# A transformer layer on one core: output inputs turned by DMA transposes instead of TensorE, output scales and last tile's products on other steps

## The chip, the cores and the metric

The kernel runs on one core of one Trainium2 chip. Its time is the device time of one execution in microseconds; before the change the median of three runs is 2656.93 us (2654.02 to 2658.84). The core has TensorE (PE in the profile; its weight loads are PEld), VectorE (DVE), ScalarE (ACT), GpSimd (POOL) and SyncE (SP), which issues nearly all DMAs of this kernel on one queue.

## What is computed

The reference is one layer of a hybrid transformer, batch 1, sequence 2048, model width 1024, and a final norm:

```python
h = _modulate(_rmsnorm(x, norm1_g), sh1, sc1)
rq, rk, rv, rg, aq, ak, av = jnp.split(h @ w_in, SPLIT_IDX, axis=-1)
...
ret, _, _ = _bidir_retention(rq_h, rk_h, _heads(rv, RET_HEADS), log_gamma, s_f, s_b)
ret = _ret_out(ret, rg, ret_gn_g)
...
att = _latent_attention(q.reshape(B, L, ATT_KV_HEADS, ATT_GROUP, ATT_HD), k, v, kc, vc)

x = x + g1 * (jnp.concatenate([ret, att], axis=-1) @ w_out)

h2 = _modulate(_rmsnorm(x, norm2_g), sh2, sc2)
x = x + g2 * _sqrelu_mlp(h2, w_ff1, w_ff2)
```

The change sits at the product with `w_out`. Its left factor is, for each row of 128 positions, 512 values of the retention (`ret`) and 512 of the attention (`att`).

## The kernel before, in words

Three stages follow each other. A projection stage (to about 606 us) makes queries, keys, values and gates, and prepares scales; the rows of the later modulation are summed there by `later_rows` at the steps of the list `at` (L1260). An attention stage (about 606 to 1470 us) computes attention, retention and the output product together. An MLP stage does the two feed-forward products to the end.

The attention stage is written out by hand: `on(k, phase, fn)` files a piece of work under step k and a phase, and the main loop runs the steps in order and in each step the phases in the order of `PHASES`: scores, piece, maximum, early, exp, cast, low, chain, pe, values, late, dma. Every engine's queue has its instructions in that order and executes them in order. A step handles one block of 128 keys of one attention group: TensorE makes the scores (`st`, L210 and L211) and a piece of the next group's row maxima (`mp`, L177 or L181); VectorE reduces that piece (`nm`, L190); ScalarE takes the exponential (L216) and in every second step casts two blocks to float16 (`phi`, L220); the float16 remainder (`plo`) is made by GpSimd (L227) or in two halves by VectorE (L229); three steps later TensorE does the product with the values (L243, L245). There are two banks for `st` and two for `mp`, so TensorE can be two blocks ahead of ScalarE and VectorE and no more.

A group takes 18 steps, a tile of 128 positions 36 steps (`RF`), and 16 tiles run from the last position to the first; tile 0 is done last (`last` in `output_tile`). Work that belongs to a tile is filed relative to its step k, and runs on into the next tile's steps. `retention` makes the retention of a tile in steps k+2 to k+20 (`mask`, L1659, in step k+4 on VectorE, from bank 0) and ends in `rets`; `combine` puts the attention of the tile into `ats` in step k+25 (L262, L263, GpSimd).

`output_tile` then does, for all but the last tile:

- `transpose`: TensorE turns the four 128x128 blocks of `ret` in step k+24 and those of `att` in step k+28 (L1812, against `ident`, float32), into a PSUM bank;
- `part`: ScalarE writes the float16 high part from that bank (`rh` in step k+26, `ah` in k+30, phase cast, L1818), VectorE the low part (`rl` in k+27, L1822; `al` in k+31, L1820; phase early), reading the bank and the high part;
- `product`: 16 pieces of three 512-column products each (L1830, L1831, L1832) at the steps `PLACES`; the first eight, for the first 512 output columns, in k+28 to k+35, the first four of them on `r`, the next four on `a`; the other eight in k+46 to k+57;
- `add` (VectorE, L1837), `square` (ScalarE, L1844), `store_x`, `root`, `norm` (GpSimd, L1857), and in steps k+68 to k+77 the transposes `transpose_x` (L1862), `modulate` (L1867), `shift_` (L1872) and the stores of the MLP's input.

The last tile uses the steps `LAST`; what its next stage needs is moved out of the events into `rest`, which the main loop of the MLP stage takes two at a time. `output_scales` (L1759) takes the largest values over all partitions and derives the scales `gns`, `sco` and `inv`, in steps 22 to 26, before the first tile (`R0` is 40). SyncE's DMAs of a step are filed in its phase dma and are issued in order; a DMA that waits for a tile holds those behind it.

Of the kernel before, what the change touches and what calls it, by code (L numbers as in the profile page):

```python
# [11 lines left out]
F32 = mybir.dt.float32  # L12
F32R = mybir.dt.float32r
F16 = mybir.dt.float16
# [42 lines left out]
def layer_kernel(ctx: ExitStack, tc: tile.TileContext, a: dict, out: bass.AP):  # L57
# [212 lines left out]
    with ExitStack() as st, tc.manual_schedule():  # L270
# [90 lines left out]
        def later_rows(j, use, at):  # L361


            x = {}

            def load(i, k):
                w = x[i, k] = raw("wmo")
                src = a["w_mod"][0, k * P : (k + 2) * P, (j + i) * 512 : (j + i + 1) * 512]
                nc.sync.dma_start(w, src.rearrange("(k p) n -> p k n", p=P))

            def add(i, k):
                w = x.pop((i, k))
                if k == 0:
                    x["acc", i] = mq.tile([P, 512], F32, name="macc", tag="mb", bufs=2)
                for r in range(2):
                    c, acc = cc[:, k + r, :1], x["acc", i]
                    if k + r == 0:
                        nc.vector.tensor_scalar_mul(acc, w[:, r], c)
                    else:
                        nc.vector.scalar_tensor_tensor(acc, w[:, r], c, acc, op0=ALU.mult, op1=ALU.add)  # L380

            def bias(i):
                if i == 0:
                    x["b"] = op.tile([P, 512], F32, name="mrow", tag="mrow", bufs=1)
                src = a["b_mod"][0, (j + i) * 512 : (j + i + 1) * 512]
                nc.sync.dma_start(x["b"][32 * i : 32 * i + 32], src.partition_broadcast(32))

            def sums(i):
                if i == 0:
                    x["ps"] = psM.tile([P, 512], F32, name="mps", tag="mps")  # L390
                mm(x["ps"][32 * i : 32 * i + 32], ones, x["acc", i], start=True, stop=True)

            def end():
                b = x["b"]
                nc.vector.tensor_tensor(b[:64], x["ps"][:64], b[:64], op=ALU.add)

            for i in range(2):
                for k in range(0, KT, 2):
                    s = at.pop(0)
                    do(s - 1, "load", load, i, k)  # L400
                    do(s, "aux", add, i, k)
                do(s + 2, "turn", sums, i)
# [854 lines left out]
        for s, (g, col, m) in enumerate(units):  # L1257
            post(s, g, col, *GROUPS[g][m], done[s])

        at = [16, 17, 18, 19, 20, 20, 21, 21, 22, 22, 39, 40, 41, 42, 44, 46, 48, 50, 52, 54, 56, 58, 60, 62]  # L1260
        at += [66, 67, 68, 69, 70, 72, 74, 76]
        for j, use in ((4, store_gate(0)), (6, turn_rows(shift2)), (8, turn_rows(scale2)), (10, store_gate(1))):
            later_rows(j, use, at)
        at = [39, 40, 41] + list(range(43, 64, 2)) + list(range(66, 84))
# [331 lines left out]

    room = ctx.enter_context(ExitStack())
    rp = pool(room, "rp", side="right")
    BUFS = {"orv": 3, "ork": 2, "okw": 2, "oo": 2, "sf": 2, "sb": 2, "ma": 2}
    wo = rp.tile([P, KT, 2, D], F16, name="wo")  # L1600

    def room_tile(tag, dtype=F32, shape=(P, 512)):
# [6 lines left out]
    def retention(k0):  # L1609
# [94 lines left out]
        for n, (d, c) in enumerate(todo):  # L1704
            k = k0 + SF * n
            on(k - 5, "dma", take, c, "rk", "rv")
            on(k - 2, "late", weigh, d, c)
            on(k, "pe", product, c, n % 2, (0, 1))
            on(k + 1, "pe", product, c, n % 2, (2, 3))
            if d == 0:  # L1710
                old, to, tag = ("f" if c == STATES else "s", c - 2), ("s", c - 1), "sf"
            else:
                old, to, tag = None if c == 1 else ("b", NT), ("b", NT - 1 + c), "sb"
            on(k + 1, "late", update, d, c, old, to, tag, (0, 1))
            on(k + 2, "late", update, d, c, old, to, tag, (2, 3))
            if d == 0:
                on(k + 3, "dma", keep_state, c - 1)
        assert k0 + SF * len(todo) <= R0
        for n in range(NT):
            c, k = NT - 1 - n, R0 + RF * n  # L1720
# [36 lines left out]
    def output_scales(k):  # L1757

        x = {}  # L1759

        def greatest():
            w = room_tile("oat")
            x["y"], x["t"], x["one"], x["m"] = w[:, :1], w[:, 1:2], w[:1, 4 : 4 + P], w[:1, 2:3]
            nc.vector.memset(x["one"], 1.0)
            nc.vector.tensor_reduce(x["y"], wmx[:, 72:], axis=AX.X, op=ALU.max, apply_absolute_value=True)

        def turn():
            x["ps"] = bank(1)
            nc.tensor.transpose(x["ps"][:1, 0], x["y"], ident)

        def whole():
            nc.vector.tensor_reduce(x["m"], x["ps"][:1, 0], axis=AX.X, op=ALU.max)

        def spread():
            x["ps"] = bank(1)
            mm(x["ps"][:, 0, :1], x["one"], x["m"], start=True, stop=True)

        def scales():
            y, t = x["y"], x["t"]
            nc.vector.tensor_copy(y, x["ps"][:, 0, :1])  # L1780
            binade(y)


            nc.vector.tensor_scalar_mul(y, y, 2.0**-10)
            nc.vector.tensor_tensor(y, y, inv, op=ALU.max)
            nc.vector.tensor_tensor(gns[:, 0:1], y, y, op=ALU.mult)
            nc.vector.tensor_scalar_mul(gns[:, 1:2], gns[:, 0:1], EPS)
            nc.vector.tensor_tensor(sco, sci[:, 7:8], y, op=ALU.mult)
            nc.vector.reciprocal(t, y)
            nc.vector.tensor_tensor(inv, inv, t, op=ALU.mult)  # L1790

        on(k, "late", greatest)
        on(k + 1, "pe", turn)
        on(k + 2, "early", whole)
        on(k + 3, "pe", spread)
        on(k + 4, "early", scales)

    PLACES = (28, 29, 30, 31, 32, 33, 34, 35, 46, 48, 49, 50, 52, 54, 55, 57)
    LAST = (23, 24, 25, 26, 30, 31, 32, 33, 31, 31, 32, 32, 34, 34, 35, 35)

    def output_tile(t, k, last):
        y = {}

        def fetch_x():
            y["x"] = xp.tile([P, D], F32, name="xr", tag="xr", bufs=XR)
            nc.sync.dma_start(y["x"], a["x"][0, t * P : (t + 1) * P, :])

        def transpose(w):
            src = (rets if w == "r" else ats).pop(t)
            y["ps"] = bank(1)  # L1810
            for q in range(4):
                nc.tensor.transpose(y["ps"][:, q], src[:, q * P : (q + 1) * P], ident)  # L1812

# [9 lines left out]

        def product(n, k):
            if k == 0:
                y["acc", n] = bank(n if last else 0, (P, 512))
            w = "ra"[k // 4]
            hi, lo = y[w, 0][:, k % 4], y[w, 1][:, k % 4]
            wh, wl = (wo[:, k, i, n * 512 : (n + 1) * 512] for i in range(2))
            mm(y["acc", n], hi, wh, start=k == 0, stop=False)  # L1830
            mm(y["acc", n], hi, wl, start=False, stop=False)  # L1831
            mm(y["acc", n], lo, wh, start=False, stop=k == KT - 1)  # L1832
# [6 lines left out]
        def square(n):  # L1839
            if n == 0:  # L1840
                y["ss"] = sm.tile([P, 2], F32, name="ss", tag="ss")
            c = slice(n * 512, (n + 1) * 512)
            junk = room_tile("oat")
            nc.scalar.activation(junk, y["x"][:, c], AF.Square, accum_out=y["ss"][:, n : n + 1])  # L1844

        def store_x():
# [10 lines left out]
            nc.gpsimd.tensor_scalar(y["x"], y["x"], y["r"], 1.0, op0=ALU.mult, op1=ALU.mult)  # L1857

        def transpose_x(q):
            y["ps", q] = bank(q if t < 2 else 1)  # L1860
            for i in range(4):
                nc.tensor.transpose(y["ps", q][:, i], y["x"][:, (4 * q + i) * P : (4 * q + i + 1) * P], ident)  # L1862

# [10 lines left out]
        def store_h(q):  # L1874
            nc.sync.dma_start(h2_d[t][:, 4 * q : 4 * q + 4], y["u", q])

        steps = (20, 21, 22, 27, 28, 30) if last else (24, 26, 27, 28, 30, 31)
        for w, at in zip("ra", (steps[:3], steps[3:])):
            on(k + at[0], "pe", transpose, w)
            on(k + at[1], "cast", part, w, 0)  # L1880
            on(k + at[2], "early", part, w, 1)
        on(k + 26, "dma", fetch_x)
        places = LAST if last else PLACES
        for j, at in enumerate(places):
# [59 lines left out]
    done = attention()  # L1944
    retention(26)
    output_weights(30)
    output_scales(22)
    for n, t in enumerate(range(NT - 1, -1, -1)):
        made_at = output_tile(t, R0 + RF * n, n == NT - 1)
    for j in range(4):  # L1950
# [447 lines left out]
    with tc.manual_schedule():  # L2398
        for k in range(min(events)[0], max(events)[0] + 1):
            for phase in PHASES:  # L2400
                run(k, phase)
                if phase in ("maximum", "low", "late"):
                    link()
        assert not events and not chain
        up_jobs()
        down_jobs()
        k = min(events)[0]
        while events:
            for phase in FPHASES:
# [67 lines left out]
```

## Time and profile before

| what | before |
|---|---|
| median of 3 runs | 2656.93 us |
| profiled execution, its own time | 2656.33 us |
| its span | 2654.5 us |
| TensorE busy in the span | 98% |
| VectorE / GpSimd / ScalarE busy | 77% / 66% / 57% |
| share of the 16 DMA engines that SyncE's queue takes | 54.8% |
| period of a tile (from one `store_x` to the next, 780 to 993 us) | 53.2 us |

The span is the time from the first to the last instruction; the execution's own time has 1.8 us beside it. A row of a timeline reads: start in us from the span's start, duration in us, engine, line of the kernel, operation, out<-in, shape, count, and in brackets the idle time of the engine before it with what ended it. Matmul rows show a modelled end; the time a matmul really costs is the distance to the next start (0.22 us for 512 columns of float16). In the list of DMAs the last number is the median time from issue to landing.

### The profile page before, as it was taken

Reading aid. Unit: us, or ns where it says so; the run is one execution under the profiler, and the core shown is the slowest. Engines: PE = TensorE matmul, PEld = TensorE weight load, DVE = VectorE, ACT = ScalarE, POOL = GpSimd, SP = SyncE. Lnnn points to the kernel's source line nnn. Section 1 sums busy time; section 2 is a strip of 40 time slices with the busy share of each in tenths; the row PEclk is TensorE's granted clock in tenths of the full one; section 3 lists DMA queues with packets and bytes.
Section 4 is the critical chain, followed back from the end, with each engine's and each line's share of the span. In section 5 each row is a group of like instructions: output and inputs, shape, how many; then the busy total and the mean of one; then the engine's idle time right before and its main releaser. Section 6 shows DMA issues by size and latency. Waiting matters only on the chain.

```text
span 2654.5 us, 45435 instructions
## 1 busy us (share of the span) xinstructions
PE 2601.0 (98%) x16617; PEld 1450.9 (55%) x16617; DVE 2049.4 (77%) x3099; ACT 1504.7 (57%) x2544; POOL 1761.7 (66%) x1451
## 2 busy tenths in 40 slices
PE   8999999998999999999999999999999999999998
PEld 5875555545666666666666444444444444444443
DVE  5778798677888888988987597889876656655686
ACT  3856343425877778788878575666665322222243
POOL 3644566545676668888887696677662666666686
PEclk9999999999999999999999999999999999999999
DMA  7876899746022123333422754776685757475453
GB/s 231 272 252 207 303 330 323 257 119 218 25 84 72 57 65 116 96 84 92 128 77 80 259 170 150 230 241 231 208 297 144 278 180 287 165 293 174 160 187 114
DMA packets 332903, 481.84 MB, mean 182 GB/s; under 512 B 90228, under 2 KB 200068, under 8 KB 328200
## 3 DMA queue, kind: packets, MB, share of 16 engines
q1 hardware_dynamic: 332664, 478.94, 54.8%
q8 instruction: 130, 2.13, 0.3%
q14 instruction: 93, 0.76, 0.1%
q10 hardware_dynamic: 16, 0.01, 0.0%
HBM read 321.89 MB, written 156.38 MB: 180 GB/s over the span
## 4 chain that ended last, share of the span: by engine, by line
PE 69%; ACT 3%; POOL 2%; DVE 1%; DMA 1%; issue 0%; SPq 0%; POOLq 0%; DVEq 0%; ACTq 0%
PE pd L2290 7%; PE pd L2289 7%; PE pd L2288 7%; PE pu L2063 7%; PE pu L2061 7%; PE pu L2062 7%; PE st L210 4%; PE o L245 4%; PE st L211 4%; PE mp L177 3%; PE o L243 2%; PE bank L1832 2%; PE bank L1830 2%; PE bank L1831 2%; ACT p L216 1%; ACT phi L220 1%
## 5 line engine op out<-in xcount | busy, mean ns | idle before, releaser
L190 DVE TENSOR_REDUCE nm<-mp 128x1 f32<-128x512 f32 x558 | 377.6, 685 | 90.7 <-PE mp L177 85.4
L216 ACT ACTIVATE p<-st 128x512 f32<-128x512 f32 x576 | 341.4, 600 | 162.7 <-PE st L211 156.3
L227 POOL TENSOR_TENSOR plo<-p,phi 128x1024 f16<-128x1024 f32 x160 | 348.2, 2181 | 87.1 <-ACT phi L220 87.0
L2063 PE MATMUL pu<-hf,w1f 128*128 128x512 f16 x896 | 339.6, 379 | 0.0
L2290 PE MATMUL pd<-w,uf 128*128 128x512 f16 x896 | 339.6, 379 | 0.0
L2061 PE MATMUL pu<-hf,w1f 128*128 128x512 f16 x896 | 339.6, 379 | 0.0
L2289 PE MATMUL pd<-w,uf 128*128 128x512 f16 x896 | 339.6, 379 | 0.0
L2062 PE MATMUL pu<-hf,w1f 128*128 128x512 f16 x896 | 339.6, 379 | 0.0
L2288 PE MATMUL pd<-w,uf 128*128 128x512 f16 x896 | 339.6, 379 | 0.0
L2308 POOL TENSOR_TENSOR y<-y,d 128x512 f32<-128x512 f32 x128 | 210.4, 1646 | 146.6 <-ACT uf L2277 99.9
L220 ACT ACTIVATE phi<-p 128x1024 f16<-128x1024 f32 x288 | 305.2, 1060 | 0.0
L229 DVE TENSOR_TENSOR plo<-p,phi 128x512 f16<-128x512 f32 x256 | 240.1, 939 | 21.8 <-ACT phi L220 9.4
L243 PE MATMUL o<-wv,plo 128*128 128x65 f16 x2304 | 230.7, 193 | 0.3 <-POOL plo L227 0.2
L245 PE MATMUL o<-wv,phi 128*128 128x129 f16 x2176 | 229.0, 220 | 0.0
L210 PE MATMUL st<-qr,ks 128*128 128x512 f16 x576 | 218.3, 379 | 8.6 <-ACT p L216 6.3
L243 PEld LDWEIGHTS <-plo 128*128 128x128 f16 x2304 | 205.5, 98 | 30.4 <-POOL plo L227 2.4
L2300 DVE SCALAR_TENSOR_TENSOR y<-pd,scy,y 128x512 f32<-128x512 f32 x160 | 116.9, 747 | 132.3 <-PE pd L2290 132.1
L211 PE MATMUL st<-qr,ks 128*128 128x512 f16 x576 | 218.5, 379 | 0.0
L2073 DVE TENSOR_TENSOR r<-pu,r 128x512 f32<-128x512 f32 x224 | 150.0, 684 | 82.8 <-PE pu L2063 58.3
L1191 PE MATMUL pso<-wf,h_l 128*128 128x512 f16 (+1 forms) x576 | 208.2, 361 | 0.0
L1192 PE MATMUL pso<-wf,h_l 128*128 128x512 f16 (+1 forms) x576 | 208.1, 361 | 0.0
L1193 PE MATMUL pso<-wf,h_l 128*128 128x512 f16 (+1 forms) x576 | 208.1, 361 | 0.0
(389 smaller groups left out, 6116.2 us busy)
## 6 DMA issues: line engine op xcount, KB each, us to landing
wm<-in_w_ff SPq DMA_DIRECT2D x64, 512.0 KB, 7.1
u<-r SPq DMA_DIRECT2D x128, 256.0 KB, 4.4
ur<-u SPq DMA_DIRECT2D x128, 256.0 KB, 5.9
y<-x SPq DMA_DIRECT2D x64, 512.0 KB, 6.5
wf<-w2f SPq DMA_DIRECT2D x112, 256.0 KB, 2.9
w<-wf SPq DMA_DIRECT2D x28, 1024.0 KB, 10.0
w1r<-in_w_ff SPq DMA_DIRECT2D x48, 512.0 KB, 5.3
x<-y SPq DMA_DIRECT2D x48, 512.0 KB, 2.6
```

What stands on the lines that cost most here:

```text
L190: nc.vector.tensor_reduce(dst, src, axis=AX.X, op=ALU.max, negate=True)
L216: nc.scalar.activation(self.p[kt // 2][:, kt % 2], self.s.pop(kt), AF.Exp, scale=HD**-0.5)
L220: nc.scalar.activation(hi, self.p[j], AF.Copy)
L227: nc.gpsimd.tensor_tensor(lo, p, hi, op=ALU.subtract)
L243: mm(o[:, : HD + 1], lo[:, i, c], v[:, : HD + 1], start=False, stop=False)
L245: mm(o, hi[:, i, c], v[:, :VW], start=False, stop=last)
L2061: mm(pu[hf, i], whi, hi, start=k == 0, stop=False)
L2062: mm(pu[hf, i], whi, lo, start=False, stop=False)
L2063: mm(pu[hf, i], wlo, hi, start=False, stop=k == 3)
L2288: mm(ps, u[:, 0, b], w[:, b, 0], start=b == 0, stop=False)
L2289: mm(ps, u[:, 0, b], w[:, b, 1], start=False, stop=False)
L2290: mm(ps, u[:, 1, b], w[:, b, 0], start=False, stop=b == 3)
```

## The change

For all tiles but the last, the two TensorE transposes go. ScalarE and VectorE now write the float16 high and low parts of `ret` and `att` as rows, from SBUF to SBUF, in `rows`, and SyncE turns each of the four 128x512 float16 tiles by a DMA transpose, in `turn`. The casts keep their steps for `a` (k+30, k+31) and for `r` (k+26, k+27); the transposes are issued in the phase dma of the same steps, and `rh`, `rl`, `ah`, `al` are now written by DMA. The first eight products move three steps on, to k+31 to k+38, and with them their `add` (to k+39) and `square`. Banks 0 and 1 change roles in `product` and `transpose_x`. The tag `oo` has one buffer instead of two, a tag `rows` is new.

The last tile keeps its TensorE transposes. Four of its products for the second half move from steps 31 and 32 to 25 to 28, so that they lie around the transposes of `a`, whose low part is now made in phase low of step 28 instead of phase early of step 30; its bank comes from the MLP's pool.

`output_scales` starts at step 39 instead of 22, and its nine small VectorE operations are spread over steps 43 to 50, those with a second tensor replaced by a multiplication with a per-partition scalar. `keep_state` is issued one step earlier, `rest` is served after the phase pe instead of late, and in `later_rows` some of the additions move by one to three steps and the two sums are made together.

```diff
-            def sums(i):
-                if i == 0:
-                    x["ps"] = psM.tile([P, 512], F32, name="mps", tag="mps")
-                mm(x["ps"][32 * i : 32 * i + 32], ones, x["acc", i], start=True, stop=True)
+            def sums():
+                ps = psM.tile([P, 512], F32, name="mps", tag="mps")
+                for i in range(2):
+                    mm(ps[32 * i : 32 * i + 32], ones, x["acc", i], start=True, stop=True)
+                x["ps"] = ps
...
-        at = [16, 17, 18, 19, 20, 20, 21, 21, 22, 22, 39, 40, 41, 42, 44, 46, 48, 50, 52, 54, 56, 58, 60, 62]
-        at += [66, 67, 68, 69, 70, 72, 74, 76]
+        at = [16, 17, 18, 19, 20, 20, 21, 21, 24, 25, 39, 40, 41, 42, 44, 46, 49, 50, 52, 54, 56, 58, 60, 62]
+        at += [66, 67, 68, 69, 70, 71, 72, 73]
...
-    BUFS = {"orv": 3, "ork": 2, "okw": 2, "oo": 2, "sf": 2, "sb": 2, "ma": 2}
+    BUFS = {"orv": 3, "ork": 2, "okw": 2, "oo": 1, "sf": 2, "sb": 2, "ma": 2}
...
-                on(k + 3, "dma", keep_state, c - 1)
+                on(k + 2, "dma", keep_state, c - 1)
...
         def scales():
-            y, t = x["y"], x["t"]
-            nc.vector.tensor_copy(y, x["ps"][:, 0, :1])
-            binade(y)
-
-
-            nc.vector.tensor_scalar_mul(y, y, 2.0**-10)
-            nc.vector.tensor_tensor(y, y, inv, op=ALU.max)
-            nc.vector.tensor_tensor(gns[:, 0:1], y, y, op=ALU.mult)
-            nc.vector.tensor_scalar_mul(gns[:, 1:2], gns[:, 0:1], EPS)
-            nc.vector.tensor_tensor(sco, sci[:, 7:8], y, op=ALU.mult)
-            nc.vector.reciprocal(t, y)
-            nc.vector.tensor_tensor(inv, inv, t, op=ALU.mult)
-
-        on(k, "late", greatest)
+            y, t, mul = x["y"], x["t"], nc.vector.tensor_scalar_mul
+            later = [
+                lambda: nc.vector.tensor_copy(y, x["ps"][:, 0, :1]),
+                lambda: binade(y),
+                lambda: nc.vector.tensor_scalar(y, y, 2.0**-10, inv, op0=ALU.mult, op1=ALU.max),
+                lambda: mul(gns[:, 0:1], y, y),
+                lambda: mul(gns[:, 1:2], gns[:, 0:1], EPS),
+                lambda: mul(sco, sci[:, 7:8], y),
+                lambda: nc.vector.reciprocal(t, y),
+                lambda: mul(inv, inv, t),
+            ]
+            for i, fn in enumerate(later):
+                on(k + 4 + i, "late", fn)
+
+        on(k, "early", greatest)
...
-    PLACES = (28, 29, 30, 31, 32, 33, 34, 35, 46, 48, 49, 50, 52, 54, 55, 57)
-    LAST = (23, 24, 25, 26, 30, 31, 32, 33, 31, 31, 32, 32, 34, 34, 35, 35)
+    PLACES = (31, 32, 33, 34, 35, 36, 37, 38, 46, 48, 49, 50, 52, 54, 55, 57)
+    LAST = (23, 24, 25, 26, 30, 31, 32, 33, 25, 26, 27, 28, 34, 34, 35, 35)
...
+        def rows(w, i):
+            if i == 0:
+                y[w] = (rets if w == "r" else ats).pop(t)
+                y[w, "rows"] = room_tile("oat" if w == "r" else "rows", F16, (P, 2, 512))
+            row = y[w, "rows"]
+            scale = inv if w == "a" else 1.0
+            if i == 0:
+                nc.scalar.activation(row[:, 0], y[w], AF.Copy, scale=scale)
+            elif w == "a":
+                nc.vector.scalar_tensor_tensor(row[:, 1], y[w], scale, row[:, 0], op0=ALU.mult, op1=ALU.subtract)
+            else:
+                nc.vector.tensor_tensor(row[:, 1], y[w], row[:, 0], op=ALU.subtract)
+
+        def turn(w, i):
+            y[w, i] = room_tile(w + "hl"[i], F16, (P, 4, P))
+            nc.sync.dma_start(y[w, i], y[w, "rows"][:, i], transpose=True)
+
...
-                y["acc", n] = bank(n if last else 0, (P, 512))
+                y["acc", n] = bank(n if last else 1 - n, (P, 512))
...
-            y["ps", q] = bank(q if t < 2 else 1)
+            y["ps", q] = bank(q if t < 2 else 0)
...
-        steps = (20, 21, 22, 27, 28, 30) if last else (24, 26, 27, 28, 30, 31)
-        for w, at in zip("ra", (steps[:3], steps[3:])):
-            on(k + at[0], "pe", transpose, w)
-            on(k + at[1], "cast", part, w, 0)
-            on(k + at[2], "early", part, w, 1)
+        for w, at in (("r", 20), ("a", 27)) if last else (("r", 26), ("a", 30)):
+            if last:
+                on(k + at, "pe", transpose, w)
+                on(k + at + 1, "cast", part, w, 0)
+                on(k + at + (2 if w == "r" else 1), "early" if w == "r" else "low", part, w, 1)
+            else:
+                on(k + at, "cast", rows, w, 0)
+                on(k + at, "dma", turn, w, 0)
+                on(k + at + 1, "early", rows, w, 1)
+                on(k + at + 1, "dma", turn, w, 1)
...
-    output_scales(22)
+    output_scales(39)
...
-                if phase == "late" and rest:
+                if phase == "pe" and rest:
```

More of the change, by code (lines that the diff above doesn't have):

```diff
@@ L401, in later_rows @@
                     do(s, "aux", add, i, k)
-                do(s + 2, "turn", sums, i)
+            do(s + 2, "turn", sums)
             for i in range(2):
@@ L1761, in greatest @@
         def greatest():
-            w = room_tile("oat")
+            w = vp.tile([P, P + 4], F32, name="os")
             x["y"], x["t"], x["one"], x["m"] = w[:, :1], w[:, 1:2], w[:1, 4 : 4 + P], w[:1, 2:3]
@@ L1795, in output_scales @@
         on(k + 3, "pe", spread)
-        on(k + 4, "early", scales)
-    PLACES = (28, 29, 30, 31, 32, 33, 34, 35, 46, 48, 49, 50, 52, 54, 55, 57)
-    LAST = (23, 24, 25, 26, 30, 31, 32, 33, 31, 31, 32, 32, 34, 34, 35, 35)
+        on(k + 3, "late", scales)
+    PLACES = (31, 32, 33, 34, 35, 36, 37, 38, 46, 48, 49, 50, 52, 54, 55, 57)
+    LAST = (23, 24, 25, 26, 30, 31, 32, 33, 25, 26, 27, 28, 34, 34, 35, 35)
     def output_tile(t, k, last):
@@ L1806, in fetch_x @@
             nc.sync.dma_start(y["x"], a["x"][0, t * P : (t + 1) * P, :])
+        def rows(w, i):
[13 more added lines that the diff above has]
+            nc.sync.dma_start(y[w, i], y[w, "rows"][:, i], transpose=True)
         def transpose(w):
             src = (rets if w == "r" else ats).pop(t)
-            y["ps"] = bank(1)
+            y["ps"] = ff["ps"].tile([P, 4, P], F32, "aps") if last and w == "a" else bank(1)
             for q in range(4):
@@ L1842, in square @@
             c = slice(n * 512, (n + 1) * 512)
-            junk = room_tile("oat")
+            junk = room_tile("oat" if n or last else "rows")
             nc.scalar.activation(junk, y["x"][:, c], AF.Square, accum_out=y["ss"][:, n : n + 1])
```

## Prediction

> **What bounds the kernel now.** I began with the page, whose first lines give each engine's share.
>
> ```profile
> PE 2601.0 (98%) x16617; PEld 1450.9 (55%) x16617; DVE 2049.4 (77%) x3099; ACT 1504.7 (57%) x2544; POOL 1761.7 (66%) x1451
> ```
>
> TensorE is busy nearly always, so a reader would pay the change for the TensorE time that it removes. That must be read in the stage where the transposes lie; next, then, the busy time by stretches: TensorE, weight loads, VectorE, ScalarE, GpSimd, clock, DMA.
>
> ```profile
> 800.00:900.00 100.00, 99.09 (x962) 66.30 (x959) 85.19 (x159) 78.94 (x132) 67.28 (x60) 1.00 0.25 75
> 1470.00:1480.00 10.00, 7.26 (x27) 2.90 (x26) 4.36 (x4) 2.74 (x4) 8.12 (x7) 0.83 1.00 407
> ```
>
> The steady tiles (first row) look bound by TensorE, with DMA idle for three quarters. But 85 and 79% are means over a tile of 36 steps, so I took one tile's timelines, engine by engine. TensorE in steps k+24, k+28 and k+31:
>
> ```profile
> 835.02 0.60 PE L1812 MATMUL bank<-ident,oo 128*128 128x128 f32 x4
> ...
> 840.22 0.60 PE L1812 MATMUL bank<-ident,ma 128*128 128x128 f32 x4
> 840.66 0.38 PE L1830 MATMUL bank<-wo,rh 128*128 128x512 f16 x1
> ...
> 845.02 0.38 PE L181 MATMUL mp<-ks,qr 128*128 128x256 f16 x2
> 845.24 0.38 PE L1830 MATMUL bank<-wo,rh 128*128 128x512 f16 x1
> ```
>
> Four transposes cost 840.66 - 840.22 = 0.44 us of TensorE. ScalarE in the same stretch:
>
> ```profile
> 833.57 1.05 ACT L220 ACTIVATE phi<-p 128x1024 f16<-128x1024 f32 x1
> 834.51 0.62 ACT L1844 ACTIVATE oat<-xr 128x512 f32<-128x512 f32 x1
> ...
> 842.43 0.68 ACT L1818 ACTIVATE ah<-bank,inv 128x512 f16<-128x512 f32 x1
> 843.99 0.60 ACT L216 ACTIVATE p<-st 128x512 f32<-128x512 f32 x1 [0.88 <-PE st L211]
> ```
>
> No row between 833.57 and 843.11 carries an idle time: ScalarE runs through, and waits for TensorE again only after `ah`. So from step k+24 to k+30, just where both groups of transposes lie, ScalarE sets the pace and TensorE's transposes fill holes. VectorE, and GpSimd beside it:
>
> ```profile
> 838.70 0.69 DVE L1822 TENSOR_TENSOR rl<-bank,rh 128x512 f16<-128x512 f32 x1
> 839.31 0.68 DVE L190 TENSOR_REDUCE nm<-mp 128x1 f32<-128x512 f32 x1
> 840.13 1.47 DVE L229 TENSOR_TENSOR plo<-p,phi 128x512 f16<-128x512 f32 x1
> 841.52 0.68 DVE L190 TENSOR_REDUCE nm<-mp 128x1 f32<-128x512 f32 x1
> 842.12 0.92 DVE L229 TENSOR_TENSOR plo<-p,phi 128x512 f16<-128x512 f32 x1
> 842.97 0.68 DVE L190 TENSOR_REDUCE nm<-mp 128x1 f32<-128x512 f32 x1
> 844.14 0.69 DVE L190 TENSOR_REDUCE nm<-mp 128x1 f32<-128x512 f32 x1 [0.50 <-PE mp L177]
> ```
>
> ```profile
> 837.83 2.13 POOL L227 TENSOR_TENSOR plo<-p,phi 128x1024 f16<-128x1024 f32 x1
> 839.95 1.12 POOL L1857 TENSOR_SCALAR xr<-xr,cy_f 128x1024 f32<-128x1024 f32 x1
> 841.03 1.47 POOL L1626 TENSOR_TENSOR okw<-ork,kd 128x512 f32<-128x512 f32 x1
> ```
>
> VectorE has no hole from 838.70 to 843.65 either. And two kinds of its instructions behave differently beside GpSimd. `rl`, with one input in PSUM, takes 0.69 in the middle of a GpSimd `plo`. The two L229, with both inputs in SBUF, end 0.53 and 0.54 us after the GpSimd instruction that was running when they began (841.60 against 839.95 + 1.12; 843.04 against 841.03 + 1.47): they were held until it was over. [...]
>
> **The change, part by part.** *Transposes removed.* 15 tiles x 2 x 0.44 = 13.2 us of TensorE. By the ScalarE rows this time is a hole afterwards, since ScalarE's work in these steps is the same (the casts keep their steps). I count 0; the ends are 0 and -13.2.
>
> *Products displaced.* Steps k+28 to k+30 lose three products of 0.65 (three matmuls of 0.22), 1.94 us, and steps k+36 to k+38, where TensorE bounds, gain them. What TensorE wins in return is the time by which it reaches step k+31 sooner. There it needs the bank that the reduction at 842.97 frees, at 843.65; then the piece (0.22), then the first product, at about 843.9 instead of 845.24: 1.3 won, 1.94 given back, +0.6 us a tile.
>
> *Low parts from SBUF.* VectorE's `rl` has two SBUF inputs now and starts while GpSimd's `plo` runs (to 839.96). If it is held as L229 is, it ends at 839.96 + 0.54 = 840.50 instead of 839.39, and the reductions behind it, which free TensorE's banks, are 1.1 late: the one that step k+31 needs ends at 844.75, the product starts at about 845.0. Held or not is worth 1.1 us a tile; I take held, as the nearest rows have both inputs in the same places. `al` comes behind the reductions that matter here; 0. Both ends stay: +0.6 and +1.7 a tile. Times 15: +9 and **+25.5 us**, of which I take the second. [...]
>
> *The `add` of the first half* (about 0.75 on VectorE) moves from step k+36 to k+39, just ahead of `mask`, on which TensorE waits in the next step. VectorE has less to do in the slower steps before; I count 0, at worst 0.75 x 15 = +11.
>
> *60 DMA transposes.* No trace row shows one. The nearest by what they do:
>
> ```profile
> h<-u SPq DMA_DIRECT2D x32, 256.0 KB, 2.0
> ```
>
> ```profile
> oqt<-qt SPq DMA_DIRECT2D x16, 256.0 KB, 5.2
> ...
> qr<-aq SPq DMA_DIRECT2D x4, 64.0 KB, 5.7
> ```
>
> The first is a store from SBUF in this stage with a quiet queue, the second a load, the third small pieces behind a burst (830 to 850 us). The transpose of `rl` stands behind the load of x (512 KB), so I take 3.5, between 2.0 and 5.7, nearer to the store. It starts at 840.5 and must land before the product at 845.0, 4.5 later: hidden; at 5.7 it costs 1.2 a tile, +18. Without the hold both ends shift alike. The Trainium skill gives two prices. "VectorE: DVE Perf Modes", section "The three transpose paths", has 1309 ns for one 128x128 block by DMA; four in a row would be 5.2 us before the landing, an estimate, and the sum some 2695. "Advanced Engine Details and Errata", section "X-Bar Transpose (TRN2)", calls such DMAs as fast as regular ones; by that they are hidden. No row decides between the two.
>
> SyncE issues them in order, so the loads of `oqt` and `okt` (step k+28), which before left at once after `store_x`, now stand behind `rl`'s transpose, until about 840.7. Landing after 5.2 us, at 845.9, they still precede their reader:
>
> ```profile
> 847.69 1.27 POOL L1650 TENSOR_TENSOR oqf<-oqt,tf 128x512 f32<-128x512 f32 x1
> ```
>
> Cover 1.8 us; 0. If it is gone, GpSimd is late by the difference, with `plo` behind it. The loads of steps k+34 and later wait for `al`, at about 846; they are for the next tile; 0. ScalarE's casts read SBUF instead of a bank at the same size; 0. Buffers (`oo`, `oat`, `rows`) and banks are free many steps ahead; 0.
>
> *Output scales.* Before the first tile VectorE is the bound:
>
> ```profile
> 612.44 0.14 DVE L1780 COPY oat<-bank 128x1 f32<-128x1 f32 x1
> ...
> 615.94 0.16 DVE L1790 TENSOR_TENSOR inv<-inv,oat 128x1 f32<-128x1 f32 x1
> ...
> 629.93 0.60 DVE L1642 SCALAR_TENSOR_TENSOR sf<-sf,cd,bank 128x128 f32<-128x128 f32 x2 [1.49 <-DMA sf<-sf]
> ```
>
> The ten operations hold it for 3.7 us, and TensorE waits. In steps 43 to 50 ten of about 0.15 us come back, some of them in holes. The earlier `keep_state` frees `sf` one step sooner, against the 1.49. It goes ahead of no load that was on time; loads behind it on SyncE set the floor. Together **-3.5**, between -1 and -5.5.
>
> *Last tile.* TensorE after the transposes of `a`:
>
> ```profile
> 1472.10 0.39 PE L1830 MATMUL bank<-wo,ah 128*128 128x512 f16 x1 [0.78 <-ACT ah L1818]
> 1472.32 0.38 PE L1831 MATMUL bank<-wo,ah 128*128 128x512 f16 x1
> 1474.66 0.39 PE L1832 MATMUL bank<-wo,al 128*128 128x512 f16 x1 [1.96 <-DVE al L1820]
> ```
>
> 0.78 + 1.96 idle, then a granted clock of 0.83 of this window (quoted above): 1.7 us of ten. Six matmuls of 0.22 now lie over the wait for `ah`, and `al` goes ahead of VectorE's weight parts. Gross -4.4; but the next weights land late anyway:
>
> ```profile
> 1487.20 11.01 DMA w1r<-in_w_ff
> ```
>
> This row of the chain that ended last is a load that also queues behind other transfers, and takes back what TensorE arrives too soon. **-3**, between 0 and -4.9. `rest` one phase earlier is within that.
>
> *Projection stage.* The same additions and sums, a few steps off, none of which TensorE's long waits name: 0, within 1.
>
> **Sum** on the profiled execution's 2656.33 (span 2654.5 and 1.8 around it; 0.6 under the median): +25.5 - 3.5 - 3 = +19, about **2675 us**. With its own bounds (+9 to +36 in the tiles) 2659 to 2692.
>
> **Rivals.** (A) *TensorE is the bound and is paid in full*: its idle time per tile stays at the 0.5 us that 99.09 of 100 leaves, because the displaced products fill holes elsewhere. 2656.3 - 13.2 - 3.5 - 3 = 2637. For it: the stretch row. Against: ScalarE without a hole in just these steps. It decides if the product of step k+31 starts by 843.3, when the 1.94 displaced is won back. Chance 0.20. (B) *The low part isn't held*, and the balance is +9 - 6.5: 2659, no difference. For: `rl` was never held so far. Against: L229. Chance 0.12. (C) *The transposes land late* and TensorE waits for `rl` in each tile: 2675 + 18 = 2693 or more. For: `qr` at 5.7 in the burst. Against: `h<-u` at 2.0. Chance 0.13. The forecast keeps 0.55.
>
> **Numbers.** 0.2% is 5.3 us, about what a measurement of this kernel can tell from no change. Slower by more: 0.55 + 0.13 = 0.68; within: 0.12; faster: 0.20. The range of 8 in 10 leaves out most of A and the far end of C: 2645 to 2704.
>
> **What would show it.** Right: the period of a tile, 53.2 before, is near 55; TensorE shows waits for `nm` or `st` of 1 to 3 us between steps k+24 and k+31; VectorE's two new subtractions last 1 to 2 us instead of 0.69 and 0.74; no wait of TensorE for the four transposes; 610 to 650 us is shorter by some 3.5. Wrong: a period under 53 (A), the subtractions under 0.9 us (B), products that wait for a DMA (C). What I would have missed then is a hole in ScalarE's or VectorE's rows that an engine ahead of its turn can use.

## The result and the profile after

The changed kernel takes **2695.57 us** (median of four runs, 2691.06 to 2698.95) against 2655.47 for the kernel before beside it (2653.94 to 2658.84): a ratio of 1.0148, 95% interval 1.0129 to 1.0167. It is slower, as forecast, but by 40 us where the forecast had 19. Its profiled execution, the longest of the four (2698.95), has a span of 2697.2, 42.7 over the 2654.5 of before. That is the late-transposes rival's time (2693), but not its reason.

The first line of the changed kernel's page, and the same stretch of steady tiles as in the prediction (TensorE, weight loads, VectorE, ScalarE, GpSimd, clock, DMA):

```profile
PE 2600.6 (96%) x16497; PEld 1435.6 (53%) x16497; DVE 2077.8 (77%) x3098; ACT 1508.9 (56%) x2544; POOL 1768.7 (66%) x1451
```

```profile
800.00:900.00 100.00, 95.30 (x905) 61.97 (x903) 82.90 (x153) 73.85 (x123) 64.42 (x59) 1.00 0.24 68
```

The 120 missing instructions of TensorE are the transposes. Its idle time in this stretch went from 0.9 of 100 us to 4.7: more than the removed work, and no other engine is busier than before. So these are waits, and TensorE's timeline places them. The program issues 576 first score matmuls (L210), one per step, in the same order in both kernels; subtracting start from start gives what each step gained or lost. Before, the score of step k+28 (the product of k+31, at 845.24, is among the prediction's rows):

```profile
839.57 0.38 PE L210 MATMUL st<-qr,ks 128*128 128x512 f16 x1
```

and the changed kernel from step k+28 to k+41 (the bracket is TensorE's idle time and what ended it):

```profile
846.36 0.38 PE L210 MATMUL st<-qr,ks 128*128 128x512 f16 x1
...
847.46 0.38 PE L210 MATMUL st<-qr,ks 128*128 128x512 f16 x1 [0.29 <-ACT p L216]
...
850.93 0.38 PE L181 MATMUL mp<-ks,qr 128*128 128x256 f16 x2 [0.64 <-DVE nm L190]
851.14 0.38 PE L1849 MATMUL bank<-wo,rh 128*128 128x512 f16 x1
...
867.40 0.38 PE L210 MATMUL st<-qr,ks 128*128 128x512 f16 x1
867.62 0.38 PE L211 MATMUL st<-qr,ks 128*128 128x512 f16 x1
868.87 0.38 PE L177 MATMUL mp<-ks,qr 128*128 128x512 f16 x1 [0.87 <-DVE nm L190]
869.51 1.13 PE L1633 MATMUL bank<-orv,okw 128*128 128x128 f32 x8 [0.27 <-PE mp L177]
```

From the score of k+28 to the product of k+31 it was 845.24 - 839.57 = 5.67 us and is 851.14 - 846.36 = 4.78: of the 2.38 us taken out there (1.94 of products, 0.44 of the second group of transposes), 0.89 is won. And there is a wait at k+41 that the prediction didn't have. Summed over the 15 tiles by these differences:

| where | change, us |
|---|---|
| steps k+28 to k+30, three products and the second group of transposes out | -21.6 |
| step k+31, wait for `nm`, in three tiles for `rl` too | +15.9 |
| steps k+36 to k+38, three products in | +30.1 |
| step k+41, wait for `nm` | +23.0 |
| all other steps, k+24 with its removed transposes among them | -0.3 |
| tiles, sum | +47.1 |
| ahead of the first score matmul, and the 36 steps after it | -0.6, -2.2 |
| last score matmul to the first MLP product; from there to the end | -4.8, +3.2 |
| span | 42.7 |

VectorE and GpSimd of the changed kernel at steps k+39 and k+40, which feed the new wait:

```profile
864.07 0.69 DVE L190 TENSOR_REDUCE nm<-mp 128x1 f32<-128x512 f32 x1 [0.55 <-PE mp L177]
865.61 0.75 DVE L1856 SCALAR_TENSOR_TENSOR xr<-bank,sco,xr 128x512 f32<-128x512 f32 x1 [0.85 <-PE bank L1851]
866.28 1.93 DVE L229 TENSOR_TENSOR plo<-p,phi 128x512 f16<-128x512 f32 x1
868.14 0.68 DVE L190 TENSOR_REDUCE nm<-mp 128x1 f32<-128x512 f32 x1
868.74 0.67 DVE L1660 TENSOR_TENSOR oat<-bank,dT 128x512 f32<-128x512 f32 x1
```

```profile
865.53 2.13 POOL L227 TENSOR_TENSOR plo<-p,phi 128x1024 f16<-128x1024 f32 x1 [1.11 <-ACT phi L220]
```

and before, the low part at the same place of the tile:

```profile
857.93 0.68 DVE L229 TENSOR_TENSOR plo<-p,phi 128x512 f16<-128x512 f32 x1
```

The add (L1856) waits 0.85 for the last displaced product and takes 0.67; the low part behind it, 0.68 long before, now starts 0.75 after GpSimd's and ends 0.5 after GpSimd's end at 867.66. The reduction is late: TensorE could have started its next piece at 867.84 (867.62 + 0.22) and starts it at 868.87, which is 1.03 of the 1.54 us that a tile loses here. The matmuls behind it (L1633) follow after 0.64 instead of 0.21, because they take the bank that `mask` (L1660) reads, and `mask`, next in VectorE's order, ends at 869.41.

### The profile page after: what moved, and what is told of

It is laid out like the page before. It is cut to its first block, busy times and chain, and to the rows that moved or that the text cites. A ratio compares the mean times of both kernels' runs of the same rounds, so it can differ in the third digit from the quotient of the medians.

```text
span 2697.2 us, 45269 instructions
## 1 busy us (share of the span) xinstructions
PE 2600.6 (96%) x16497; PEld 1435.6 (53%) x16497; DVE 2077.8 (77%) x3098; ACT 1508.9 (56%) x2544; POOL 1768.7 (66%) x1451
## 4 chain that ended last, share of the span: by engine, by line
PE 75%; DVE 11%; DMA 6%; ACT 3%; issue 2%; POOL 2%; SPq 0%; ACTq 0%; DVEq 0%; POOLq 0%
PE pd L2312 7%; PE pd L2314 7%; PE pd L2313 7%; PE pu L2087 7%; PE pu L2085 7%; PE pu L2086 7%; PE pso L1192 3%; PE pso L1193 3%; PE pso L1194 3%; DVE plo L229 3%; PE o L245 3%; PE st L210 3%; PE st L211 3%; DVE nm L190 3%; PE mp L177 3%
## 5 line engine op out<-in xcount | busy, mean ns | idle before, releaser
L229 DVE TENSOR_TENSOR plo<-p,phi 128x512 f16<-128x512 f32 x256 | 243.5, 952 | 18.4 <-ACT phi L220 9.9
L210 PE MATMUL st<-qr,ks 128*128 128x512 f16 x576 | 218.2, 379 | 20.8 <-ACT p L216 20.4
L177 PE MATMUL mp<-ks,qr 128*128 128x512 f16 x512 | 194.1, 379 | 21.5 <-DVE nm L190 18.9
L1192 PE MATMUL pso<-wf,h_l 128*128 128x512 f16 (+1 forms) x576 | 208.1, 361 | 0.0
L1194 PE MATMUL pso<-wf,h_l 128*128 128x512 f16 (+1 forms) x576 | 208.1, 361 | 0.0
```

The source lines that it names most:

```text
L229: nc.vector.tensor_tensor(lo[:, i], p[:, i], hi[:, i], op=ALU.subtract)
```

## The experiments

Each run is given with its median, its ratio to the kernel before beside it, and the time from the first to the last score matmul ("tiles": 854.3 us before, 899.2 in the changed kernel). The second is the sharper: the projection stage ahead of it ended anywhere between 600.1 and 606.7 us in these profiles, though most of the kernels share it, while steps of the tiles repeat to 0.01 us.

**The add behind the low part** (from the changed kernel):

```
-            on(at, "early", add, n)
+            on(at, "early" if n or last else "late", add, n)
```

> The changed kernel with one line different: the add of the first half of an output tile (step k+39) stands on VectorE behind the attention low part of its step instead of ahead of it. Theory W (a wait and a hold at step k+39): in the changed kernel VectorE waits there 0.85 us for the last displaced product, adds for 0.67, and the low part behind it then falls into a GpSimd low part and lasts 1.93 instead of 0.68; TensorE loses 1.54 us in each of 15 tiles. Moved, the low part runs at once, the step k+41 interval loses its 1.54, and the time falls by about 23 us to about 2672. Theory D (the displaced products alone are the cost, wherever the add stands): TensorE meets the same wait one step on, time within 5 us of 2695. Theory T (DMA transposes arrive late): no change, 2695.

Measured 2671.26 us, ratio 1.0063 (1.0050 to 1.0075), tiles 873.3. The 1.54 us at k+41 are gone in each tile, 23.0 in sum; of the other 2.9, 2.1 lie in the 36 steps ahead of the 15 tiles.

```profile
854.50 0.68 DVE L229 TENSOR_TENSOR plo<-p,phi 128x512 f16<-128x512 f32 x1
855.43 0.75 DVE L1856 SCALAR_TENSOR_TENSOR xr<-bank,sco,xr 128x512 f32<-128x512 f32 x1 [0.25 <-PE bank L1851]
```

The low part now begins ahead of GpSimd's, which starts at 855.36 here, and isn't held. Theory W stands; D and T fall.

**Only the products moved** (from the kernel before):

```
-    PLACES = (28, 29, 30, 31, 32, 33, 34, 35, 46, ...
+    PLACES = (31, 32, 33, 34, 35, 36, 37, 38, 46, ...
-                y["acc", n] = bank(n if last else 0, (P, 512))
+                y["acc", n] = bank(n if last else 1 - n, (P, 512))
-            y["ps", q] = bank(q if t < 2 else 1)
+            y["ps", q] = bank(q if t < 2 else 0)
```

> The kernel before with only the products of the first half moved from steps k+28..35 to k+31..38 (accumulators in the banks of the changed kernel); the transposes stay on TensorE, there is no DMA transpose, and output scales and last tile are as before. Theory W: the wait and hold at step k+41 appear as in the changed kernel, +1.5 us a tile, and three displaced products cost 1.94 less what is won at step k+31, where TensorE now waits for al on VectorE: +2.0 to 3.0 us a tile in all, 2656 + 30 to 45 = 2686 to 2701. Theory T (late DMA transposes are the main cost): near +0.6 a tile, about 2665.

Measured 2703.97 us, ratio 1.0184 (1.0170 to 1.0198), tiles 901.6, slightly over what was expected. The same +1.54 stands at k+41 with no DMA transpose in the program: their landing is not the main cost. The 15 tiles lose 47.0 us, where the changed kernel's lose 47.1: 22.3 at k+41 and 24.7 around the moved products, of which 13.2 are waits of TensorE at k+31 for `al`, whose bank the first product now writes. The whole is dearer than the changed kernel because the gains ahead of the tiles and at the last one are missing.

**One SBUF input instead of two**, to part the wait from the hold at k+39, and to price the hold of `rl`. The first two attempts used a scalar multiply:

```
+            elif self.n % 2 == 0 and self.n > 1 and (j, i) == (8, 1):
+                nc.vector.tensor_scalar_mul(lo[:, i], p[:, i], 2.0**-12)
```

```
-                nc.vector.tensor_tensor(row[:, 1], y[w], row[:, 0], op=ALU.subtract)
+                nc.vector.tensor_scalar_mul(row[:, 1], y[w], 2.0**-12)
```

> The changed kernel, the add still ahead of the attention low part at step k+39, but that one low part (one 128x512 in each tile) made from one SBUF input; its subtraction of the high part is left out. It parts the two halves of the new cost at step k+41. Theory H (the hold decides: GpSimd's low part keeps VectorE's for 1.9 us): the low part takes 0.7 us or less behind the same 0.85 us wait for the product, TensorE's reduction is ready before TensorE wants its bank, and the 1.54 us a tile go; about 2672, like the run with the add moved. Rival (the in-order wait for the product and the add themselves decide): at least 1 us of the 1.54 stays, 2688 to 2696.

> The changed kernel with the low part of the retention rows made from one SBUF input (a multiple of the row; the subtraction of the high part is left out). Theory H (the hold of this low part by GpSimd's low part is what delays the reductions of steps k+28 to k+30): it lasts 0.7 us or less instead of 1.77, the 0.80 us that TensorE waits for nm at step k+31 goes, the DMA transpose of rl leaves 1.1 earlier and its late landings go too; 0.8 to 1.1 us a tile, 12 to 17 us, to about 2680. Rival: the reductions are late for ScalarE or for the next low part, which GpSimd holds anyway; then under 0.3 us a tile, 2691 to 2696.

Measured 2688.59 us, ratio 1.0124 (1.0110 to 1.0138), tiles 894.3, and 2691.00 us, ratio 1.0136 (1.0122 to 1.0150), tiles 894.7. Read by the expectations alone both would speak for the rivals, but the edit didn't do what it was for. The low part of the first, with GpSimd's beside it:

```profile
858.95 1.67 DVE L229 TENSOR_SCALAR plo<-p 128x512 f16<-128x512 f32 x1
```

```profile
858.20 2.13 POOL L227 TENSOR_TENSOR plo<-p,phi 128x1024 f16<-128x1024 f32 x1 [1.11 <-ACT phi L220]
```

It ends 0.29 after GpSimd's. In all 15 tiles it lasts 1.67 to 1.92 and ends 0.27 to 0.29 after GpSimd's: held, with one SBUF input. `rl` lasted 1.68 likewise. The Trainium skill, page "SBUF — State Buffer", section "Who interferes with whom", says that copies, casts and tensor_scalar can enter a mode that takes the port shared with GpSimd, and that a tensor_reduce never contends on this chip; the first half agrees with the 1.67. So both were run again with a reduction over an axis of one, which writes the same shape:

```
+                nc.vector.tensor_reduce(lo[:, i], p[:, i].unsqueeze(2), axis=AX.X, op=ALU.max)
```

> The changed kernel with the one attention low part behind the add at step k+39 written by a reduction over an axis of one (one SBUF input, the subtraction of the high part left out); the run with a scalar multiply in its place was held by GpSimd all the same (1.67 us). Theory H (at step k+41 the hold behind GpSimd's low part decides): the row takes 0.7 us, TensorE's wait for nm there goes, 1.54 us a tile, about 2672. Rival (the wait for the last product and the add decide): 1.0 or more of the 1.54 stays, 2686 to 2692.

> The changed kernel with the low part of the retention rows written by a reduction over an axis of one (one SBUF input, the subtraction left out); the scalar multiply tried before was still held (1.68 us). Theory P (the prediction's: the hold is worth 1.1 us a tile): the row takes 0.7 us, TensorE reaches the product of step k+31 1.1 us earlier, 16 us less, about 2679. Theory S (two holds in series: VectorE's next attention low part waits for GpSimd's next instruction in any case, and takes back what the first gave): the low part behind it grows from 1.0 to about 1.5 us, TensorE gains 0.25 to 0.4 a tile, 4 to 6 us, about 2690.

*At k+39*: 2675.88 us, ratio 1.0068 (1.0056 to 1.0080), tiles 877.7.

```profile
857.93 0.75 DVE L1858 SCALAR_TENSOR_TENSOR xr<-bank,sco,xr 128x512 f32<-128x512 f32 x1 [0.85 <-PE bank L1853]
858.60 0.68 DVE L229 TENSOR_REDUCE plo<-p 128x512 f16<-128x512 f32 x1
```

The wait of 0.85 and the add are unchanged, the low part is short while GpSimd's runs (from 857.85), and 19.1 of the 23.0 us go. The wait for the product mainly makes the low part late enough to be held: the hold is five sixths of the price, and the other 3.9 us stay with the wait and the add. The reduction's 0.68 also bears out the second half of the rule quoted from the Trainium skill.

*`rl`*: 2684.32 us, ratio 1.0104 (1.0091 to 1.0117), tiles 887.3: 11 us off, between the two theories. Its rows at k+27 and k+28, and GpSimd's:

```profile
837.49 0.68 DVE L1821 TENSOR_REDUCE oat<-oo 128x512 f16<-128x512 f32 x1
838.08 0.68 DVE L190 TENSOR_REDUCE nm<-mp 128x1 f32<-128x512 f32 x1
839.09 1.44 DVE L229 TENSOR_TENSOR plo<-p,phi 128x512 f16<-128x512 f32 x1 [0.33 <-ACT phi L220]
```

```profile
836.75 2.13 POOL L227 TENSOR_TENSOR plo<-p,phi 128x1024 f16<-128x1024 f32 x1
838.87 1.12 POOL L1876 TENSOR_SCALAR xr<-xr,cy_f 128x1024 f32<-128x1024 f32 x1
```

and the changed kernel's:

```profile
845.52 1.77 DVE L1821 TENSOR_TENSOR oat<-oo,oat 128x512 f16<-128x512 f32 x1
847.22 0.68 DVE L190 TENSOR_REDUCE nm<-mp 128x1 f32<-128x512 f32 x1
847.82 1.01 DVE L229 TENSOR_TENSOR plo<-p,phi 128x512 f16<-128x512 f32 x1
```

```profile
846.73 1.56 POOL L1876 TENSOR_SCALAR xr<-xr,cy_f 128x1024 f32<-128x1024 f32 x1
```

With `rl` free the attention low part behind it is held for 1.44 by GpSimd's next instruction; with `rl` held for 1.77 it takes 1.01. Two holds in series: in the nine steady tiles the second takes back all but 0.25 us of the 1.1 at k+29 and k+30, and with k+31 these tiles gain 0.4 on average. In the four tiles with MLP work on GpSimd the reduction won 0.88 at k+29 but only 0.4 to 0.7 in all; in the first and the last tile it won 1.8 and 1.9. The hold also goes the other way: GpSimd's next instruction takes 1.12 here and in the kernel before, and 1.56 in the changed kernel, where it starts while VectorE's late `rl` still runs. TensorE, earlier now, waits more often for the transpose to land; the waits for it in the changed kernel, then in this one (us in total, times, longest):

```profile
PE bank L1851 <- DMA rl<-oat: 1.4, 3, 0.7
```

```profile
PE bank L1851 <- DMA rl<-oat: 3.8, 6, 1.7
```

**The load of x behind the transposes** (from the changed kernel):

```
-        on(k + 26, "dma", fetch_x)
+        on(k + (26 if last else 28), "dma", fetch_x)
```

> The changed kernel with the load of x (512 KB) issued two steps later, behind the transposes of rh and rl instead of between them. Theory L (rl lands late in some tiles because its transpose queues behind that load): TensorE's waits for rl at step k+31 (0.2 to 0.9 us in five of fifteen tiles of the changed kernel) go, 3 to 6 us, about 2690. Rival (the transpose itself is slow or held by other transfers): the waits stay, 2694 to 2697.

Measured 2693.91 us, ratio 1.0143 (1.0129 to 1.0157), tiles 895.7. The mechanism is right: the waits for `rl` are gone, and its row in the list of DMAs, median from issue to landing, changes from the first to the second line:

```profile
rl<-oat SPq DMA_TRANSPOSE x15, 3.8
```

```profile
rl<-oat SPq DMA_TRANSPOSE x15, 2.4
```

But it is worth 2.0 us by the steps, not 3 to 6: the waits were in three tiles, not five. In the first and the last tile it is `nm` that is later, and that stays.

**Old output tiles, the rest of the change kept** (from the changed kernel; PE transposes, PLACES, banks, buffers and tags as before):

```
+            for w, at in zip("ra", ((24, 26, 27), (28, 30, 31))):
+                on(k + at[0], "pe", transpose, w)
+                on(k + at[1], "cast", part, w, 0)
+                on(k + at[2], "early", part, w, 1)
```

> The changed kernel with the output tiles as before (TensorE transposes, products at steps k+28..35, the add at k+36, the same banks and buffers); what stays of the change is the output scales on steps 39 to 50, the last tile, the earlier state store and the small moves of the projection stage. Theory W: all of the loss lies in the 15 tiles, so this is faster than before by the 2 to 3 us seen at the first tile and some 1.6 at the last: 2651 to 2653. Rival: moved output scales or the last tile cost something later that the tiles cover; then 2656 or more.

Measured **2645.91 us**, ratio 0.9967 (0.9955 to 0.9979), tiles 851.4: faster than both, and further below than expected. Of the 6.5 us between the two spans, 2.2 lie ahead of the first score matmul (in the spread of that stage), 2.8 in the 36 steps after it, and 4.8 - 3.3 behind the last score matmul. No step of the 15 tiles moved by 0.1.

**DMA transposes, but early, with the products in their old places** (from the changed kernel, PLACES as before):

```
-        for w, at in (("r", 20), ("a", 27)) if last else (("r", 26), ("a", 30)):
+        for w, at in (("r", 20), ("a", 27)) if last else (("r", 22), ("a", 28)):
-            junk = room_tile("oat" if n or last else "rows")
+            junk = room_tile("oat" if last else "rows")
```

> The changed kernel with its DMA transposes kept, but the casts and turns of the retention rows from step k+22 and of the attention rows from k+28, and the products back at k+28..35 with the add at k+36 (square's spare output in another buffer, so that no buffer of the turns is overwritten). Theory W+D (the loss is the displaced products and the add at k+39, not the DMA transposes): both go, and the time falls to that of the kernel with the old output tiles, 2646, or up to 7 us below it, since the second group of TensorE transposes (0.44 us at k+28) is gone: 2639 to 2648. Theory T (a DMA transpose delays what needs it, or the loads queued behind it on SyncE): TensorE waits for rl or al at k+28 or k+32 by 0.4 us or more in each tile, 2652 to 2665.

Measured 2651.97 us, ratio 0.9987 (0.9978 to 0.9996), tiles 855.8. That lies between the two expected ranges, but no tile waits for a transpose, so theory T is out. TensorE wins the 0.44 of the second group at k+28 in every tile, gives 0.14 back at k+31, and comes out 1.5 us behind in the four tiles with more work on GpSimd, where `rl`'s low part lasted 2.0 us. So moving it one step on:

> The run with early turns (2652) with the low part of the retention rows and its transpose one step later, at k+24. In four tiles, where GpSimd is about 2 us later, that low part was held for 2.0 us and TensorE lost 1.4 us; if that hold is the cause, these four lose it, about 6 us, and 2644 to 2648 follows. Rival: rl then lands too late for the product of step k+28, or meets another hold; 2650 or more.

Measured 2648.94 us, ratio 0.9968 (0.9956 to 0.9980), tiles 850.5. In those four the low part still lasts 1.4, but what TensorE loses from k+25 to k+27 falls from 0.84 to 0.24; the steady tiles keep the full 0.44. In the four TensorE still waits 0.81 more at k+31. It ties with the old output tiles: its 15 tiles take 0.1 us more in all. This run and the one before it keep the changed kernel's banks, so the exchanged banks alone aren't the loss either.

**Only the attention rows by DMA** (from the kernel with old output tiles): `rows` and `turn` for `a` at k+28 and k+29, `r` on TensorE.

> From the kernel with old output tiles (2646): only the attention rows by DMA transposes, cast and turned from step k+28, low part at k+29; the retention rows stay on TensorE, in the hole of step k+24, and their low part reads PSUM; products at k+28..35 and the add at k+36. If the holes and holds are read rightly, the 0.44 us of TensorE at k+28 is won but for up to 0.15 at k+31, in all 15 tiles: 4 to 7 us less, 2639 to 2642. Rival: al lands too late for the product of step k+32 or is held by GpSimd in the tiles with more work on it; then 2645 to 2652.

Measured 2656.52 us, ratio 1.0001 (0.9992 to 1.0009), tiles 860.5, outside both expected ranges. The 0.44 at k+28 is won, and 1.65 is lost at k+31 in eight of the 15 tiles; this is the same trap as the add's. VectorE's row behind the new low part of `a`, and GpSimd's:

```profile
833.81 0.92 DVE L1819 SCALAR_TENSOR_TENSOR rows<-ma,inv,rows 128x512 f16<-128x512 f32 x1
834.66 2.61 DVE L229 TENSOR_TENSOR plo<-p,phi 128x512 f16<-128x512 f32 x1
```

```profile
834.39 2.34 POOL L227 TENSOR_TENSOR plo<-p,phi 128x1024 f16<-128x1024 f32 x1 [0.20 <-ACT phi L220]
```

The attention low part comes 0.27 too late and is held for 2.61.

**Both mixed**: early DMA transposes in ten tiles, TensorE's in five.

> From the kernel with old output tiles (2646): both kinds of rows by early DMA transposes, the low part of the retention rows at k+24, in ten tiles; TensorE transposes as before in the five tiles where the run with all turned early lost at step k+31 (tile 1 and the four with more work on GpSimd). By the step intervals of that run each of nine or ten steady tiles wins the 0.44 us of TensorE at step k+28 and loses nothing elsewhere: 4 us less, 2640 to 2643. Rival: a hold moves to another step when the tiles alternate; then 2645 or more.

Measured 2647.12 us, ratio 0.9972 (0.9961 to 0.9983), tiles 850.6: the rival's number, for a plain reason. An output tile stands one tile behind the score matmuls of the same step, and the five were taken one off: the four tiles with the wait at k+31 kept it (0.82), and four of the five tiles given back to TensorE were steady ones. In one tile TensorE also waited 0.6 for the transpose of `ah` to land. What the right choice would bring wasn't tried.

## Why the prediction was wrong in size

- **The add, costed at 0 "at worst 0.75 x 15 = +11", was 23.0 us**, and this is the step that failed. It was priced by its own length. But VectorE also stands still in front of it until the product is done (0.85), and behind it in VectorE's order comes a low part with two SBUF inputs. The prediction had the hold, with two L229 rows to show it, and applied it to the new subtractions only, not to the old instructions that the move pushes later. With 23 in that place the sum is 42 and the time 2698.
- **Displaced products** (+9) and **hold of `rl`** (+16.5): together 25.5 forecast; measured 47.1 - 23.0 = 24.1, which includes 2.0 for late `rl`. The sum was right, the parts less so: without the hold the 15 tiles are 9.9 us shorter (37.2 over before instead of 47.1), and would be 12.3 but for 2.4 more of waiting for the landing. So in the changed kernel the hold is worth 10 to 12, and what is left for the products is 10 to 12. The forecast took the hold as 1.1 in each tile; in the steady tiles it is 0.4 on average, since the next hold absorbs most of it, 0.4 to 0.7 in the four with MLP work and 1.8 to 1.9 in the first and the last. That such a sum of parts came out is in part luck: with only the products moved there is no such hold, and the same steps cost 24.7, because another wait, for `al`, stands in its place.
- **Transposes removed, 0**: right for the first group; interval k+24 didn't change by 0.1 us in any steady tile. The second group doesn't lie in a hole. The prediction took ScalarE's rows without a wait for the bound up to k+30, but the last wait of TensorE for ScalarE ends here, one score ahead of k+28:

```profile
838.23 0.38 PE L210 MATMUL st<-qr,ks 128*128 128x512 f16 x1 [0.32 <-ACT p L216]
```

  From there to the product at 845.24 TensorE has no wait, and early turns win the whole 0.44. In the changed kernel that gain doesn't show: its interval k+28 is 0.63 shorter, and with the products alone moved it is 0.65 shorter.
- **DMA transposes hidden**: right but for three tiles and 2.0 us. (The "some 2695" given beside the sum for a landing of 5.2 us doesn't follow from the cover of 4.5: that leaves 0.7 a tile, about 2685.) Rival C gave about the time that came and is false: the kernel without DMA transposes has the same new wait.
- **Output scales -3.5**: these 36 first steps are 2.2 us shorter in the changed kernel and 2.4 to 6.1, mostly about 4, in the eleven runs that share the moved scales; in the run without them they are 0.4 longer. What makes this spread stays open, and no run parts the scales from the earlier `keep_state`. **Last tile -3**: -4.8 until the first MLP product, and 3.2 given back, as the load that the prediction named now takes 14.32 us instead of 11.01.

```profile
1528.46 14.32 DMA w1r<-in_w_ff
```

- The expected signs: the tile period, from one `store_x` to the next, is 55.8 to 56.9 rather than 55; the subtractions did last 1.4 to 1.8 in most tiles (up to 2.6), and TensorE waited for `nm`. These came true while the largest cost stood elsewhere. The bounds 2659 to 2692 set the lower end of the tiles beside the middle of the gains; with the gains' own upper ends (5.5 and 4.9) the lower bound is about 2655.

## What to carry to other kernels

Price a moved instruction by what it pushes, not by its length: list the instructions behind it on its engine until the next slack, and ask of each whether it now starts on the wrong side of another engine's instruction that can hold it. In these runs an instruction that waits for TensorE did best behind those that were ready, and a chain that was held twice by the same engine paid little more than once in the steady tiles. And when an edit is to take a suspected hold away, look first at whether its own row got shorter; only then read the time.

## What the runs showed of the hardware

- A VectorE multiply by a scalar from one fp32 SBUF input to fp16 was held by GpSimd like a subtraction of two (1.67 and 1.68 us), a reduction over an axis of one was not (0.68). The multiply ended 0.27 to 0.29 us after GpSimd's instruction, the subtractions of two SBUF inputs shown here 0.53 to 0.55 after it.
- Order decides: the same 0.68 us low part ran unhindered when it began ahead of GpSimd's, and took 1.93 when it began 0.75 behind it.
- A DMA transpose of 128x512 fp16 lands 2.4 to 2.5 us after its issue (medians) when nothing large is ahead of it, but holds SyncE's queue for 1.2 us, two to four times as long as the plain DMAs around it (0.33 to 0.61):

```profile
845.51 1.23 SPq L1825 DMA_TRANSPOSE rh<-oat  x1
846.79 0.58 SPq L1808 DMA_DIRECT2D xr<-in_x  x1
847.48 1.20 SPq L1825 DMA_TRANSPOSE rl<-oat  x1
```

The price of 1309 ns for one 128x128 block in the Trainium skill, page "VectorE: DVE Perf Modes", section "The three transpose paths", would make 5.2 us for such four, an estimate; the landings of 2.4 us speak against adding it up block by block.
